# A decoder layer on one core: the gating's first factor moves from channel tiles to a ninth unit of seven-product block multiplication

## The chip, the cores and the metric

The kernel runs on one core of one Trainium2 chip. The core has TensorE (PE, matrix products; PEld is its weight load), VectorE (DVE), ScalarE (ACT), GpSimd (POOL) and SyncE (SP, whose queue issues the DMAs). Each engine works through its own instructions in order and waits for the others by semaphores. The metric is the device time of one execution in microseconds (us).

## The reference

One decoder layer with three gated branches, D_MODEL 2048, 256 positions, 256 memory tokens, all in float32. The part that the change touches is the branch with the spatial gating unit:

```python
proj = x @ w_in
q_a, k_a, v_a, z_a, u_g, v_g, z_g, q_c, z_c, g_logit = split(proj)
v = layer_norm(gelu(v_g));  mixed = masked 128x128 position mixing of v, + b_s
y_g = gelu(u_g) * mixed * silu(z_g)
merged = gates[0] * (y_a @ w_branch_attn) + gates[1] * (y_g @ w_branch_sgu) + gates[2] * (y_c @ w_branch_mem)
out = layer_norm(ALPHA * x + merged @ w_out)
```

`u_g`, the gating's first factor, is `x` (256 x 2048) times 1024 columns of `w_in`. The other two branches are attention over 8 heads (`q_a`, `k_a`, `v_a`, `z_a`) and cross-attention to the memory (`q_c`, `z_c`).

## The kernel before

Every product keeps nearly full float32 accuracy: each operand is split into a rounded part `hi` (a copy on ACT, L62) and a rest `lo` (a subtraction on DVE, L63), and the products hi*hi, hi*lo, lo*hi are summed in PSUM. So each weight that PE reads has passed ACT and DVE first.

Two streams of work share PE.

**The channel tiles** ("C"). A tile of 128 output columns (`channel_tile`) streams both parts of `x` past stationary weights: 16 steps of one 512-column matmul (hi, L190) and one 256-column matmul (lo, L191). Its weights come as one 1 MB chunk in `raw`, split in two halves of 1024 columns. `zc`, `qc`, `za`, `q`, `k`, `ug` and `zg` are eight such tiles each; `mv`, `mk` (the memory's values and keys) and the three gated branches `b` (12 matmuls of 512 columns in a half chunk) run on chunks too. PSUM tiles of these come from `acc`, three buffers.

**The block units** ("S"). A unit computes 1024 columns of `x @ w_in` as 2 x 2 blocks with seven products, M1 M5 M6 M3 M7 M4 M2. Each product is two steps (h = 0, 1) of 12 matmuls of 512 columns (L391 to L393), so a unit is 14 steps, numbered through all units. A step needs its block split into `sh` (ACT) and `sl` (DVE), 2048 columns each. Six steps of a unit need an in-place difference of two blocks on DVE first (`s_sum`, L312), and M3 two more (L325). The pool `shl` has four tiles, two pairs: the pair for step s + 2 can be written only when step s has left PE. Four results of a unit (128 x 512) are finished by an addition on DVE (L351). There are eight units: six for the merge gates, unit 2 for `v_a`, unit 5 for `v_g`.

The small matmuls of attention, memory attention, position mixing and the transposes of the merged result take turns in `aux`, two PSUM buffers. A buffer is reused in the order in which the program asks for one, so a tile waits for the tile two requests ahead. An attention head goes through three stages, scores (`s`), transposes (`pt`), values (`o`), one at each `tick` (one per finished C tile). The 256-wide work tiles (`q`, `k`, gates, halves of sums) share eight buffers `w1`.

What sets the order: `pace` assigns, from a table of DVE costs, how many S steps follow each C half (0 to 2), and `DUE` sets the latest places of whole units. The recorded program then passes a scheduler that builds each engine's final order, so S steps and C halves are interleaved matmul by matmul on PE. The first blocks of unit 0 are loaded as riders on given chunks (`riders`), among the loads of `mv` and `mk`.

At the end `u`, the GELU of `ug`, is multiplied into the mixed tile in `sgu_gate`, together with the SiLU of `zg`.

Of the kernel before, what the change touches and what calls it, by code (L numbers as in the profile page):

```python
# [10 lines left out]
AF = mybir.ActivationFunctionType  # L11
# [13 lines left out]


@with_exitstack
def decoder_layer(ctx, tc, xT, memT, x_tok, w_st, w_mv, w_mk, w_zc, w_qc, w_za, w_qk, w_ug, w_zg,
                  w_br, w_o, w_sT, sgu_bc, ln_g, ln_b, out):
    nc = tc.nc  # L30

# [10 lines left out]
    def w2(name, shape=(P, 512)):  # L42
        return work.tile(list(shape), F32, tag="w2", name=name, bufs=6)
# [4 lines left out]
    def spill(name, shape, dt=F32):  # L48
        return dram.tile(list(shape), dt, tag=name, name=name)
# [111 lines left out]
    chunks += [w_br[2 * 8 + j] for j in range(8)]  # L161
    chunks += [w_za[j] for j in range(3, 8)]
    chunks += [w_qk[j] for j in range(16)]
    chunks += [w_ug[j] for j in range(3)]
    chunks += [w_br[j] for j in range(8)]
    chunks += [w_ug[j] for j in range(3, 8)]
    chunks += [w_zg[j] for j in range(8)]
    chunks += [w_br[8 + j] for j in range(8)]

    def held(i, kh):  # L170
# [114 lines left out]

    UNITS = 8
    PRODUCTS = ("M1", "M5", "M6", "M3", "M7", "M4", "M2")
    FORM = {"M5": 1, "M6": 2, "M3": 4, "M7": 3}  # L290
    rt, shl, xsf, sp = {}, {}, {}, {}
# [161 lines left out]
    def run(gen):  # L453
# [5 lines left out]
        while left[0]:  # L459
# [1 line left out]
            yield  # L461

    first = lambda blk, h: lambda: s_load(0, blk, h)
    riders.update({4: [x_loads[0]], 5: [first(B12, 0)], 6: [x_loads[1]], 7: [first(B12, 1)],
                   10: [first(B11, 0)], 12: [first(B11, 1)]})
    for _ in run(mem_values()):
        pass
    for i, _ in enumerate(run(mem_keys())):
        if x_work:
            x_work.pop(0)()  # L470
        if i in (12, 14):
            riders[ptr["load"]] = [first(B22, i // 2 - 6)]
    while x_work:
        x_work.pop(0)()
        step(lambda: None)
# [20 lines left out]
                store(d[j], v)  # L496
            yield from channel_tile(x_k, f"{w}{j}", fin)

    szc_d, sza_d, gu_d = ([spill(f"{n}{j}", (P, S)) for j in range(8)] for n in ("szc", "sza", "gu"))


    MSC = float(2 * P) ** -0.5
# [148 lines left out]
    def sgu_gate(j):  # L651
        st = {}

        def fetch():
            st["c"] = w2(f"sc{j}", (P, 3, P))
            st["w"] = w1(f"ws{j}", (P, P))
            st["u"] = w1(f"gu{j}")
            nc.sync.dma_start(st["c"], sgu_bc[j].partition_broadcast(P))
            nc.sync.dma_start(st["w"], w_sT[:, j * P:(j + 1) * P])
            nc.sync.dma_start(st["u"], gu_d[j])  # L660
            nc.gpsimd.affine_select(out=st["w"], in_=st["w"], compare_op=ALU.is_ge,
                                    fill=0.0, base=0, pattern=[[1, P]], channel_multiplier=-1)

        def scale():
            v = vg[0][:, :, j * P:(j + 1) * P]
            for i, op in ((0, ALU.mult), (1, ALU.add)):
                nc.vector.tensor_tensor(v, v, st["c"][:, i][:, None, :].to_broadcast([P, 2, P]), op=op)

        def mix(z):
            ps = new_aux(f"mix{j}", (P, 2, P))  # L670
            for c in range(2):
                nc.tensor.matmul(ps[:, c], vg[0][:, c, j * P:(j + 1) * P], st["w"], start=(c == 0), stop=(c == 1),
                                 skip_group_check=True)
            m = w1(f"m{j}", (P, 2, P))
            nc.vector.tensor_tensor(m, ps, st["c"][:, 2][:, None, :].to_broadcast([P, 2, P]), op=ALU.add)
            m2 = m.rearrange("p c t -> p (c t)")
            nc.vector.tensor_tensor(m2, m2, st["u"], op=ALU.mult)
            nc.vector.tensor_tensor(m2, m2, z, op=ALU.mult)
            put_y(1, j, m2)

        return fetch, scale, mix

    def gating():
        for j in range(8):
            fetch, scale, mix = sgu_gate(j)
            fetch()

            def fin(ps, j=j, scale=scale, mix=mix):
                scale()
                z = w1(f"zg{j}")  # L690
                joined(z, ps, f"zg{j}")
                nc.scalar.activation(z, z, AF.Silu)
                pending.append([lambda: None, lambda: mix(z)])
            yield from channel_tile(x_k, f"zg{j}", fin)

# [64 lines left out]

    GATES = {0: (2, 0), 1: (2, 1), 3: (0, 0), 4: (0, 1), 6: (1, 0), 7: (1, 1)}

    def classic():
        yield from gate_tiles("zc", AF.Silu, szc_d)
        new_y(2)
        yield from mem_attention()
        yield from gate_tiles("za", AF.Silu, sza_d, range(3))
        yield from gated_branch(2, 0)
        yield from gate_tiles("za", AF.Silu, sza_d, range(3, 8))
        new_y(0)  # L770
        yield from block_attention()
        yield from gate_tiles("ug", AF.Gelu_apprx_tanh, gu_d, range(3))
        yield from gated_branch(0, 1)
        yield from gate_tiles("ug", AF.Gelu_apprx_tanh, gu_d, range(3, 8))
        new_y(1)
        yield from gating()
        yield from gated_branch(1, 2)

    S_STEPS = 14 * UNITS
    KINDS = ([(16, 1.2), (16, 1.75), (6, 1.2), (16, 1.3), (10, 1.2), (32, 1.65), (6, 1.2), (16, 1.6), (10, 1.2),
              (16, 2.2), (16, 1.9)])
    C_COST = [cost for n, cost in KINDS for _ in range(n)]
    DUE = {38: 14, 46: 28, 64: 42, 102: 56, 110: 70, 126: 84, 144: 98, 152: 112}
# [70 lines left out]
    for t in range(2):  # L856
        for i, c0 in enumerate((1536, 1792)):
# [83 lines left out]
```

## Time and profile before

| | |
|---|---|
| three runs: median (lowest to highest) | 997.91 us (997.07 to 998.18) |
| the profiled execution, its time | 1001.29 us |
| its span, first to last instruction | 999.5 us |
| PE busy | 977.3 us (98%) |
| DVE busy | 816.4 us (82%) |
| ACT busy | 592.8 us (59%) |
| HBM traffic over the span | 269 GB/s |
| TensorE clock granted, mean | 0.992 |

A busy share counts an instruction from its start to its end. Matmuls are pipelined: one of 512 columns is shown with 0.39 us, but the next starts 0.23 us later, so costs on PE are read as distances between starts. DVE instructions overlap by about 0.09 us in the same manner. A row of a timeline gives start, length, engine, line, operation, tiles written and read, and in brackets the idle time of the engine just before it and what ended it.

### The profile page before, as it was taken

Reading aid. Unit: us, or ns where it says so; the run is one execution under the profiler, and the core shown is the slowest. Engines: PE = TensorE matmul, PEld = TensorE weight load, DVE = VectorE, ACT = ScalarE, POOL = GpSimd, SP = SyncE. Lnnn points to the kernel's source line nnn. Section 1 sums busy time; section 2 is a strip of 40 time slices with the busy share of each in tenths; the row PEclk is TensorE's granted clock in tenths of the full one; section 3 lists DMA queues with packets and bytes.
Section 4 is the critical chain, followed back from the end, with each engine's and each line's share of the span. In section 5 each row is a group of like instructions: output and inputs, shape, how many; then the busy total and the mean of one; then the engine's idle time right before and its main releaser. Section 6 shows DMA issues by size and latency. Waiting matters only on the chain.

```text
span 999.5 us, 12911 instructions
## 1 busy us (share of the span) xinstructions
PE 977.3 (98%) x4888; PEld 824.2 (82%) x4888; DVE 816.4 (82%) x776; ACT 592.8 (59%) x669; POOL 6.4 (1%) x17
## 2 busy tenths in 40 slices
PE   9999999999999999999999999999999999999995
PEld 7778888888888888888888888877877888878885
DVE  5954998897689789788987988899899876676647
ACT  5644665546686565665566567886555557544520
POOL 0000000000000000000000000000000000000000
PEclk9999999999999999999999999999999999999998
DMA  9998579648974896697579468847986956868622
GB/s 334 405 397 322 208 254 397 230 174 290 339 260 159 332 400 229 241 348 269 178 289 363 143 238 322 311 162 304 404 304 216 342 176 207 284 234 320 227 82 84
DMA packets 68125, 269.28 MB, mean 269 GB/s; under 512 B 7520, under 2 KB 21600, under 8 KB 45536
## 3 DMA queue, kind: packets, MB, share of 16 engines
q1 hardware_dynamic: 68064, 268.47, 73.0%
q8 instruction: 38, 0.62, 0.2%
q14 instruction: 23, 0.19, 0.1%
HBM read 245.37 MB, written 23.07 MB: 269 GB/s over the span
## 4 chain that ended last, share of the span: by engine, by line
PE 86%; DVE 5%; ACT 4%; issue 3%; DMA 1%; SPq 0%; DVEq 0%; ACTq 0%
PE sM L392 9%; PE sM L391 9%; PE sM L393 9%; PE b L717 4%; PE b L718 4%; PE b L716 3%; PE mk L190 3%; PE zc L190 3%; PE za L190 3%; PE q L190 3%; PE qc L190 3%; PE zg L190 3%; PE o L824 3%; PE o L825 3%; PE o L823 3%; PE mv L429 3%
## 5 line engine op out<-in xcount | busy, mean ns | idle before, releaser
L63 DVE TENSOR_TENSOR lo<-raw,hi 128x1024 fp32r<-128x1024 f32 (+1 forms) x218 | 262.6, 1213 | 74.3 <-ACT hi L62 72.6
L62 ACT ACTIVATE hi<-raw 128x1024 fp32r<-128x1024 f32 (+1 forms) x218 | 227.0, 1048 | 156.2 <-PE o L825 31.9
L63 DVE TENSOR_TENSOR sl<-b,sh 128x2048 fp32r<-128x2048 f32 x112 | 256.1, 2290 | 53.3 <-ACT sh L62 53.1
L62 ACT ACTIVATE sh<-b 128x2048 fp32r<-128x2048 f32 x112 | 214.4, 1914 | 125.0 <-PE sM L392 107.5
L312 DVE TENSOR_TENSOR b<-b,b 128x2048 f32<-128x2048 f32 x48 | 109.8, 2288 | 9.9 <-DMA b<-in_w_st_dram 9.9
L392 PE MATMUL sM<-sl,xf 128*128 128x512 f32 x256 | 101.3, 396 | 0.9 <-DVE sl L63 0.9
L391 PE MATMUL sM<-sh,xf 128*128 128x512 f32 x256 | 100.7, 393 | 1.4 <-ACT sh L62 1.3
L393 PE MATMUL sM<-sh,xf 128*128 128x512 f32 x256 | 100.3, 392 | 0.0
L717 PE MATMUL b<-lo,yhl 128*128 128x512 f32 x192 | 75.4, 393 | 0.8 <-DVE lo L63 0.8
L391 PE MATMUL sM<-sh,xhl 128*128 128x512 f32 x192 | 75.7, 394 | 0.0
L392 PE MATMUL sM<-sl,xhl 128*128 128x512 f32 x192 | 75.5, 393 | 0.0
L393 PE MATMUL sM<-sh,xhl 128*128 128x512 f32 x192 | 75.0, 390 | 0.0
L718 PE MATMUL b<-hi,yhl 128*128 128x512 f32 x192 | 74.5, 390 | 0.0
L716 PE MATMUL b<-hi,yhl 128*128 128x512 f32 x192 | 72.2, 391 | 0.0
L391 PEld LDWEIGHTS sM<-sh,xf 128*128 128x128 f32 x256 | 48.1, 188 | 12.3 <-ACT sh L62 2.4
L392 PEld LDWEIGHTS sM<-sl,xf 128*128 128x128 f32 x256 | 48.1, 188 | 11.5 <-DVE sl L63 1.6
L393 PEld LDWEIGHTS sM<-sh,xf 128*128 128x128 f32 x256 | 48.1, 188 | 9.9
L190 PE MATMUL mk<-memhl,hi 128*128 128x512 f32 x128 | 46.1, 402 | 1.6 <-ACT hi L62 1.6
L190 PE MATMUL ug<-xhl,hi 128*128 128x512 f32 x128 | 47.3, 406 | 0.0
L190 PE MATMUL q<-xhl,hi 128*128 128x512 f32 x128 | 46.8, 399 | 0.0
L190 PE MATMUL k<-xhl,hi 128*128 128x512 f32 x128 | 46.7, 399 | 0.0
L190 PE MATMUL qc<-xhl,hi 128*128 128x512 f32 x128 | 46.1, 399 | 0.0
(295 smaller groups left out, 1886.2 us busy)
## 6 DMA issues: line engine op xcount, KB each, us to landing
b<-in_w_st_dram SPq DMA_DIRECT2D x64, 1024.0 KB, 7.4
xf<-xf SPq DMA_DIRECT2D x64, 512.0 KB, 5.3
raw<-in_w_br_dram SPq DMA_DIRECT2D x24, 1024.0 KB, 5.2
raw<-in_w_qk_dram SPq DMA_DIRECT2D x16, 1024.0 KB, 7.0
raw<-in_w_o_dram SPq DMA_DIRECT2D x16, 1024.0 KB, 4.9
raw<-in_w_mk_dram SPq DMA_DIRECT2D x8, 1024.0 KB, 9.1
raw<-in_w_zc_dram SPq DMA_DIRECT2D x8, 1024.0 KB, 5.5
raw<-in_w_qc_dram SPq DMA_DIRECT2D x8, 1024.0 KB, 6.4
```

The source lines that it names most:

```text
L62: nc.scalar.activation(hi, v, AF.Copy)
L63: nc.vector.tensor_tensor(lo, v, hi.bitcast(F32), op=ALU.subtract)
L190: nc.tensor.matmul(ps, hi, x, start=first, stop=False)
L312: nc.vector.tensor_tensor(o, rt[u, other, h], o, op=ALU.subtract)
L391: nc.tensor.matmul(ps, ah, hi[:, c], start=first, stop=False, skip_group_check=True)
L392: nc.tensor.matmul(ps, ah, lo[:, c], start=False, stop=False, skip_group_check=True)
L393: nc.tensor.matmul(ps, al, hi[:, c], start=False, stop=last, skip_group_check=True)
L429: nc.tensor.matmul(ps[t][n], lhs, rhs[:, n * 512:(n + 1) * 512], start=(k == 0 and rhs is hi and lhs is xh[t]), stop=(k == KT - 1 and lhs ...
L716: nc.tensor.matmul(ps[t], yh, hi[:, c], start=(k == 0), stop=False)
L717: nc.tensor.matmul(ps[t], yh, lo[:, c], start=False, stop=False)
L718: nc.tensor.matmul(ps[t], yl, hi[:, c], start=False, stop=(k == 7))
L823: nc.tensor.matmul(ps[:, 0:n], mh, hi, start=first, stop=False)
```

## The change

`ug` is no longer eight channel tiles. Its 1024 columns become unit 6 of the block units, between `v_g` and the gates of the gating branch, so there are 9 units and 126 S steps instead of 8 and 112. A unit's results have positions on the partitions, and the gating wants channels there, so each of the four results (128 x 512) is transposed on PE in four 128 x 128 pieces into an `aux` tile (`channel_major`), GELU is applied as ACT reads it, and it is stored. `sgu_gate` fetches it in two pieces and multiplies it into the SiLU of `zg` (`both`) instead of into the mixed tile.

Where `ug`'s first three tiles stood, ahead of the gated branch 0, `zg`'s first three tiles are computed now, stored in `szg`, and fetched again in `gating` (`behind`); `gating` computes the other five.

The table of the pace, the due places and the tail limit are set anew, and unit 0's first blocks ride on other chunks.

```diff
-    riders.update({4: [x_loads[0]], 5: [first(B12, 0)], 6: [x_loads[1]], 7: [first(B12, 1)],
-                   10: [first(B11, 0)], 12: [first(B11, 1)]})
+    riders.update({4: [x_loads[0]], 6: [x_loads[1]], 9: [first(B12, 0)], 11: [first(B12, 1)],
+                   13: [first(B11, 0)], 14: [first(B11, 1)], 16: [first(B22, 0)], 17: [first(B22, 1)]})
...
-        if i in (12, 14):
-            riders[ptr["load"]] = [first(B22, i // 2 - 6)]
...
-            nc.vector.tensor_tensor(m2, m2, st["u"], op=ALU.mult)
...
+        def both(z):
+            nc.vector.tensor_tensor(z, z, st["u"], op=ALU.mult)
...
+        elif u == 6:
+            late.append(lambda: channel_major(t, n, r))
...
+    def channel_major(t, n, r):
+        ps = new_aux(f"uT{t}{n}", (P, 4, P))
+        for i in range(4):
+            nc.tensor.transpose(ps[:, i], r[:, i * P:(i + 1) * P], ident)
+        v = w2(f"uv{t}{n}", (P, 4, P))
+        nc.scalar.activation(v, ps, AF.Gelu_apprx_tanh)
+        store(gu_d[t, n], v)
...
-        yield from gate_tiles("ug", AF.Gelu_apprx_tanh, gu_d, range(3))
+        yield from gate_tiles("zg", AF.Silu, szg_d, range(3))
         yield from gated_branch(0, 1)
-        yield from gate_tiles("ug", AF.Gelu_apprx_tanh, gu_d, range(3, 8))
...
-    DUE = {38: 14, 46: 28, 64: 42, 102: 56, 110: 70, 126: 84, 144: 98, 152: 112}
+    DUE = {38: 14, 46: 28, 64: 42, 102: 56, 110: 70, 114: 84, 118: 98, 128: 112, 136: 126}
```

Three places show what becomes of the order. Names end in a buffer number; a line of the kernel after stands one lower than the same line before.

ACT, where `mv` ends and `mk` begins, before (`mvs` is the copy of a finished `mv` tile, `hi8_0` the first half of `mk`'s first chunk):

```order
L62 ACTIVATE xw10_782<-F10_749 128x4x128
L62 ACTIVATE xw11_807<-F11_750 128x4x128
L439 ACTIVATE mvs01_491<-mv01_122 128x512
L439 ACTIVATE mvs11_495<-mv11_124 128x512
L62 ACTIVATE hi8_0_434<-raw8_344 128x1024
L62 ACTIVATE hi8_1_450<-raw8_344 128x1024
```

and now:

```order
L62 ACTIVATE xw11_809<-F11_752 128x4x128
L62 ACTIVATE hi8_0_430<-raw8_340 128x1024
L62 ACTIVATE hi8_1_446<-raw8_340 128x1024
L438 ACTIVATE mvs01_489<-mv01_122 128x512
L62 ACTIVATE hi9_0_467<-raw9_376 128x1024
```

Both halves of `mk`'s first chunk have moved ahead of the two copies that wait for the last `mv` matmuls.

PE, around S steps 82 to 84, before (`ug2` is a C tile, `o6`, `s7` belong to attention heads 6 and 7):

```order
L392 MATMUL sM2_5_5382<-sl82_5305,xhl_96 128x512
...
L190 MATMUL ug2_5449<-xhl_96,hi66_1_5399 128x512
L191 MATMUL ug2_5449<-xhl_96,lo66_1_5400 128x256
L608 MATMUL o6_5315<-ptT6_5245,vah6_5147 128x256
...
L579 MATMUL s7_5321<-kT7_5059,qT7_5058 128x256
L392 MATMUL sM2_5_5382<-sl83_5353,xhl_96 128x512
...
L391 MATMUL sM1_6_5475<-sh84_5395,xhl_96 128x512
L190 MATMUL ug2_5449<-xhl_96,hi66_1_5399 128x512
```

and now, from the end of `k6` to the first matmul of `q7`, the next C tile:

```order
L390 MATMUL sM2_5_4564<-sh82_4484,xhl_96 128x512
...
L190 MATMUL k6_5505<-xhl_96,lo61_1_5428 128x256
L391 MATMUL sM2_5_4564<-sl82_4485,xhl_96 128x512
...
L390 MATMUL sM1_6_4673<-sh93_5056,xf93_5054 128x512
L778 MATMUL uT01_5134<-ident_83,k6_6_4997 128x128 x4
L599 MATMUL pt3_5163<-ident_83,p3_5074 128x128 x3
L390 MATMUL sM4_6_5236<-sh94_5154,xhl_96 128x512
...
L606 MATMUL o3_5258<-ptT3_5167,vah3_5085 128x256
...
L390 MATMUL sM4_6_5236<-sh95_5205,xhl_96 128x512
L189 MATMUL q7_5601<-xhl_96,hi62_0_5506 128x512
```

Steps 82 to 94, thirteen of them, stand in one piece, with no C matmul between; the transposes of head 3 stand behind `uT01`, the first transposes of the new unit, and `q7` behind both.

DVE, between the splits of steps 85 and 88, before (`lo68`, `lo69` are halves of C chunks):

```order
L312 TENSOR_TENSOR b0_6_1_5263<-b1_6_1_5122,b0_6_1_5263 128x2048
L63 TENSOR_TENSOR sl86_5492<-b0_6_0_5193,sh86_5491 128x2048
L640 BN_STATS vst_5472<-vg_5174 128x6
L63 TENSOR_TENSOR lo68_0_5564<-raw68_5403,hi68_0_5563 128x1024
L211 TENSOR_TENSOR ug2_5536<-ug2_5449,ug2l_5537 128x256
L63 TENSOR_TENSOR lo68_1_5617<-raw68_5403,hi68_1_5616 128x1024
L325 TENSOR_TENSOR b1_6_1_5122<-b2_6_1_5356,b1_6_1_5122 128x2048
L63 TENSOR_TENSOR lo69_0_5653<-raw69_5499,hi69_0_5652 128x1024
L312 TENSOR_TENSOR b0_6_0_5193<-b2_6_0_5308,b0_6_0_5193 128x2048
L644 BN_AGGR vmv_5473<-vst_5472 128x2
L63 TENSOR_TENSOR sl87_5533<-b0_6_1_5263,sh87_5532 128x2048
```

and now:

```order
L324 TENSOR_TENSOR b1_6_0_4267<-b2_6_0_4488,b1_6_0_4267 128x2048
L63 TENSOR_TENSOR sl86_4690<-b0_6_0_4356,sh86_4689 128x2048
L311 TENSOR_TENSOR b0_6_1_4400<-b1_6_1_4312,b0_6_1_4400 128x2048
L642 BN_AGGR vmv_4672<-vst_4671 128x2
L311 TENSOR_TENSOR b0_6_0_4356<-b2_6_0_4488,b0_6_0_4356 128x2048
L324 TENSOR_TENSOR b1_6_1_4312<-b2_6_1_4528,b1_6_1_4312 128x2048
L217 TENSOR_SCALAR vgv_4847<-vmv_4672 128x2
L63 TENSOR_TENSOR sl87_4731<-b0_6_1_4400,sh87_4730 128x2048
L63 TENSOR_TENSOR sl88_4793<-b0_6_0_4356,sh88_4792 128x2048
```

The halves of C chunks have left this stretch; splits of S steps and differences of blocks follow each other directly.

## Rows read from the trace of the kernel before

**Rows 1.** Stretches: length, busy time of engines, clock, DMA share (columns in the header).

```profile
core 0: us, PE busy (x) PEld busy (x) DVE busy (x) ACT busy (x) POOL busy (x), PEclk, DMA share, GB/s
101.00:605.40 504.40, 504.40 (x2536) 427.07 (x2535) 438.51 (x351) 314.88 (x351) 0.00 (x0) 1.00 0.73 266
647.40:734.00 86.60, 84.61 (x371) 68.43 (x370) 82.66 (x71) 59.27 (x61) 0.00 (x0) 1.00 0.79 307
734.00:786.40 52.40, 49.41 (x246) 41.34 (x245) 50.70 (x45) 30.39 (x30) 0.00 (x0) 0.97 0.74 261
```

**Rows 2.** Groups by line: operation, tiles, count, busy us, mean ns, idle before.

```profile
L63 DVE TENSOR_TENSOR sl<-b,sh 128x2048 fp32r<-128x2048 f32 x112 | 256.1, 2290 | 53.3 <-ACT sh L62 53.1
L62 ACT ACTIVATE sh<-b 128x2048 fp32r<-128x2048 f32 x112 | 214.4, 1914 | 125.0 <-PE sM L392 107.5 <-DVE b L312 7.6 <-PE sM L393 4.4
L312 DVE TENSOR_TENSOR b<-b,b 128x2048 f32<-128x2048 f32 x48 | 109.8, 2288 | 9.9 <-DMA b<-in_w_st_dram 9.9
L190 PE MATMUL ug<-xhl,hi 128*128 128x512 f32 x128 | 47.3, 406 | 0.0
L351 DVE TENSOR_TENSOR k<-sM,k 128x512 f32<-128x512 f32 x32 | 22.0, 686 | 2.5 <-PE sM L393 2.3
```

**Rows 3.** Timeline of PE: distances between starts in each kind of work.

```profile
642.77 0.39 PE L190 MATMUL ug<-xhl,hi 128*128 128x512 f32 x1
...
644.17 0.40 PE L190 MATMUL ug<-xhl,hi 128*128 128x512 f32 x1
...
746.28 0.39 PE L391 MATMUL sM<-sh,xf 128*128 128x512 f32 x1
...
747.64 0.39 PE L391 MATMUL sM<-sh,xf 128*128 128x512 f32 x1
...
904.57 1.03 PE L744 MATMUL mT<-ident,sg 128*128 128x128 f32 x8
905.36 0.48 PE L824 MATMUL o<-lo,mhl 128*128 128x512 f32 x1
```

**Rows 4.** PE and ACT where mk begins, the clock behind it, mk's first loads.

```profile
51.37 0.61 PE L429 MATMUL mv<-hi,memhl 128*128 128x512 f32 x2
53.62 0.49 PE L190 MATMUL mk<-memhl,hi 128*128 128x512 f32 x1 [1.63 <-ACT hi L62]
54.88 0.39 PE L191 MATMUL mk<-memhl,lo 128*128 128x256 f32 x1 [0.76 <-DVE lo L63]
...
51.12 0.60 ACT L439 ACTIVATE mvs<-mv 128x512 f32<-128x512 f32 x1 [4.18 <-PE mv L429]
...
52.52 1.05 ACT L62 ACTIVATE hi<-raw 128x1024 fp32r<-128x1024 f32 x1
...
56.00:60.00 4.00, 4.00 (x15) 3.42 (x15) 1.09 (x1) 1.03 (x1) 0.00 (x0) 0.59 1.01 404
...
L125 SPq DMA_DIRECT2D raw<-in_w_mk_dram x3: 328/332/333, 37.3 to 48.2; - x3
...
DMA to landing us min/median/max: 5.3/10.4/11.3
```

**Rows 5.** PE and DVE around PE's longest wait, and the clock behind it.

```profile
751.38 0.39 PE L191 MATMUL ug<-xhl,lo 128*128 128x256 f32 x1 [2.67 <-DVE lo L63]
...
743.17 2.29 DVE L63 TENSOR_TENSOR sl<-b,sh 128x2048 fp32r<-128x2048 f32 x1
745.37 2.29 DVE L325 TENSOR_TENSOR b<-b,b 128x2048 f32<-128x2048 f32 x1
...
750.10 1.23 DVE L63 TENSOR_TENSOR lo<-raw,hi 128x1024 fp32r<-128x1024 f32 x1
...
753.03 0.63 PE L190 MATMUL ug<-xhl,hi 128*128 128x512 f32 x1
...
754.31 0.63 PE L190 MATMUL ug<-xhl,hi 128*128 128x512 f32 x1
...
753.00:755.00 2.00, 2.00 (x9) 1.71 (x8) 2.00 (x2) 0.00 (x0) 0.00 (x0) 0.50 0.59 115
```

More of the change, by code (lines that the diff above doesn't have):

```diff
@@ L27, in decoder_layer @@
 @with_exitstack
-def decoder_layer(ctx, tc, xT, memT, x_tok, w_st, w_mv, w_mk, w_zc, w_qc, w_za, w_qk, w_ug, w_zg,
+def decoder_layer(ctx, tc, xT, memT, x_tok, w_st, w_mv, w_mk, w_zc, w_qc, w_za, w_qk, w_zg,
                   w_br, w_o, w_sT, sgu_bc, ln_g, ln_b, out):
@@ L163, in decoder_layer @@
     chunks += [w_qk[j] for j in range(16)]
-    chunks += [w_ug[j] for j in range(3)]
+    chunks += [w_zg[j] for j in range(3)]
     chunks += [w_br[j] for j in range(8)]
-    chunks += [w_ug[j] for j in range(3, 8)]
-    chunks += [w_zg[j] for j in range(8)]
+    chunks += [w_zg[j] for j in range(3, 8)]
     chunks += [w_br[8 + j] for j in range(8)]
@@ L283, in decoder_layer @@
     x_loads, x_work = x_stages()
-    UNITS = 8
+    UNITS = 9
     PRODUCTS = ("M1", "M5", "M6", "M3", "M7", "M4", "M2")
@@ L497, in gate_tiles @@
             yield from channel_tile(x_k, f"{w}{j}", fin)
-    szc_d, sza_d, gu_d = ([spill(f"{n}{j}", (P, S)) for j in range(8)] for n in ("szc", "sza", "gu"))
+    szc_d, sza_d, szg_d = ([spill(f"{n}{j}", (P, S)) for j in range(8)] for n in ("szc", "sza", "szg"))
+    gu_d = {(t, n): spill(f"gu{t}{n}", (P, 4, P)) for t in range(2) for n in range(2)}
     MSC = float(2 * P) ** -0.5
@@ L654, in fetch @@
         def fetch():
-            st["c"] = w2(f"sc{j}", (P, 3, P))
-            st["w"] = w1(f"ws{j}", (P, P))
+            sc = w2(f"sc{j}", (P, 4, P))
+            st["c"], st["w"] = sc[:, 0:3], sc[:, 3]
             st["u"] = w1(f"gu{j}")
@@ L659, in fetch @@
             nc.sync.dma_start(st["w"], w_sT[:, j * P:(j + 1) * P])
-            nc.sync.dma_start(st["u"], gu_d[j])
+            for t in range(2):
+                nc.sync.dma_start(st["u"][:, t * P:(t + 1) * P], gu_d[t, j // 4][:, j % 4])
             nc.gpsimd.affine_select(out=st["w"], in_=st["w"], compare_op=ALU.is_ge,
@@ L676, in mix, with behind, fin @@
             m2 = m.rearrange("p c t -> p (c t)")
-            nc.vector.tensor_tensor(m2, m2, st["u"], op=ALU.mult)
             nc.vector.tensor_tensor(m2, m2, z, op=ALU.mult)
             put_y(1, j, m2)
-        return fetch, scale, mix
+        def both(z):
+            nc.vector.tensor_tensor(z, z, st["u"], op=ALU.mult)
+        return fetch, scale, both, mix
     def gating():
-        for j in range(8):
-            fetch, scale, mix = sgu_gate(j)
+        def behind(j):
+            fetch, scale, both, mix = sgu_gate(j)
             fetch()
-            def fin(ps, j=j, scale=scale, mix=mix):
+            z = w1(f"szg{j}")
+            nc.sync.dma_start(z, szg_d[j])
+            pending.append([lambda: (scale(), both(z)), lambda: mix(z)])
+        for j in range(3, 8):
+            fetch, scale, both, mix = sgu_gate(j)
+            fetch()
+            if j < 6:
+                late.append(lambda j=j: behind(j - 3))
+            def fin(ps, j=j, scale=scale, both=both, mix=mix):
                 scale()
@@ L692, in fin @@
                 nc.scalar.activation(z, z, AF.Silu)
+                both(z)
                 pending.append([lambda: None, lambda: mix(z)])
@@ L759, in s_finish @@
                 pending.append(sgu_norm())
-    GATES = {0: (2, 0), 1: (2, 1), 3: (0, 0), 4: (0, 1), 6: (1, 0), 7: (1, 1)}
+    def channel_major(t, n, r):
[5 more added lines that the diff above has]
+        store(gu_d[t, n], v)
+    GATES = {0: (2, 0), 1: (2, 1), 3: (0, 0), 4: (0, 1), 7: (1, 0), 8: (1, 1)}
     def classic():
@@ L781, in decoder_layer @@
     S_STEPS = 14 * UNITS
-    KINDS = ([(16, 1.2), (16, 1.75), (6, 1.2), (16, 1.3), (10, 1.2), (32, 1.65), (6, 1.2), (16, 1.6), (10, 1.2),
-              (16, 2.2), (16, 1.9)])
+    KINDS = ([(16, 1.2), (16, 1.75), (6, 1.2), (16, 1.3), (10, 1.2), (32, 1.65), (6, 1.9), (16, 1.8), (10, 2.2),
+              (16, 1.9)])
     C_COST = [cost for n, cost in KINDS for _ in range(n)]
-    DUE = {38: 14, 46: 28, 64: 42, 102: 56, 110: 70, 126: 84, 144: 98, 152: 112}
+    DUE = {38: 14, 46: 28, 64: 42, 102: 56, 110: 70, 114: 84, 118: 98, 128: 112, 136: 126}
     S_COST = 3.2
@@ L801, in decoder_layer @@
     share = 0.80
-    while pace(share)[1] < S_STEPS or sum(pace(share)[0][:148]) < S_STEPS:
+    while pace(share)[1] < S_STEPS or sum(pace(share)[0][:134]) < S_STEPS:
         share += 0.005
@@ L863, in decoder_layer @@
         normalise(t)
-_ARGS = ['xT', 'memT', 'x_tok', 'w_st', 'w_mv', 'w_mk', 'w_zc', 'w_qc', 'w_za', 'w_qk', 'w_ug', 'w_zg',
+_ARGS = ['xT', 'memT', 'x_tok', 'w_st', 'w_mv', 'w_mk', 'w_zc', 'w_qc', 'w_za', 'w_qk', 'w_zg',
          'w_br', 'w_o', 'w_sT', 'sgu_bc', 'ln_g', 'ln_b']
@@ L902, in _layout @@
         "x_tok": a["x"].reshape(2, P, D),
-        "w_st": np.stack([blocks(w) for w in (gate(2, 0), gate(2, 1), col(2), gate(0, 0), gate(0, 1), col(5),
+        "w_st": np.stack([blocks(w) for w in (gate(2, 0), gate(2, 1), col(2), gate(0, 0), gate(0, 1), col(5), col(4),
                                               gate(1, 0), gate(1, 1))]),
@@ L910, in _layout @@
         "w_qk": np.stack([q, k], 1).reshape(16, P, D),
-        "w_ug": stat(col(4)),
         "w_zg": stat(col(6)),
```

## Prediction

> **What bounds the kernel now.** First the table of stretches [rows 1]: from 101 to 605 us PE is busy for the whole 504.4 us while DVE is busy for 438.5 (87%). PE is the bound there and loses nothing to waits, though DVE has only 13% to spare. The next two stretches differ: from 647 to 734 PE stands idle for 2.0 us (86.60 less 84.61) with DVE at 95%, and from 734 to 786 for 3.0 us (52.40 less 49.41) with DVE at 97%. So DVE becomes the bound wherever the work that PE asks of it is dense, and PE waits there. The timeline shows one case [rows 5]: `lo` of a `ug` half stands behind a row of 2048-wide splits and differences, starts at 750.10, and PE waits 2.67 us for it; afterwards the granted clock is 0.50, which is 1.2 instead of 2.4 GHz. The other loss lies where `mv` gives way to `mk` [rows 4].
>
> **Costs of one piece.** On PE a pair of a C step costs 0.35 us (four pairs between 642.77 and 644.17), a matmul of an S step 0.227 us (six between 746.28 and 747.64), a transpose 0.10 us (eight between 904.57 and 905.36) [rows 3]. An S step, 12 matmuls, is thus 2.73 us of PE. On DVE a 2048-wide operation lasts 2.29 us, but the next starts 2.20 us later (743.17 to 745.37) [rows 2, 5]; taking off the same 0.09, a `lo` costs 1.14 (1.23 in [rows 5]) and a result's addition 0.60 (0.686 in [rows 2]). A unit has 14 splits, 8 differences and 4 additions: 22 times 2.20 plus 4 times 0.60 is 50.8 us of DVE, or 3.63 per step. That is more than the 2.73 of PE that the step gives: S steps can run at PE's speed only mixed with C steps, which cost PE 2.80 per half and DVE only 1.14 and a little.
>
> **The change, part by part.**
>
> *The work on PE.* Away go 128 pairs of `ug`, counted in [rows 2]: 128 times 0.35 is 44.8 us. New are 14 steps of 2.73, 38.2 us, and 16 transposes of 0.10, 1.6 us. Sum: -5.0 us, on the path wherever PE is the bound. The bounds are -5.5 (transposes hidden) and -2.4 (a transpose at the 0.26 us that is left of its busy time if nothing overlaps, from the 1.03 of [rows 3]).
>
> The Trainium skill, "TensorE: Matmul & The Clock Gate", Part 4, gives about 275 ns for a transpose in a kernel's context. Here eight start within 0.79 us, so by the trace they overlap; with the page's figure 16 would cost 4.4 us and this item would be -2.2.
>
> *The order where `mk` begins.* Before, ACT copies two `mv` tiles, idle for 4.18 us until PE has finished them, and only then rounds `mk`'s first chunk at 52.52. PE starts a matmul at 51.60 and the next at 53.62: 1.8 us lost; the following one at 54.88: 1.0 lost; then the clock is at 0.59 for 4 us, some 1.5 lost [rows 4]. Sum 4.3. Now both halves stand ahead of the copies. Their data was there even before: the load issued at 37.3 landed at the latest 11.3 us on, at 48.6 [rows 4], and 2 MB of riders are now behind it. I take -4.3; bounds -4.5 and -2.
>
> *The waits between 647 and 787.* They sum to 5.0 us of idle PE [rows 1], and the half clock behind the longest costs some 1.4 (a clock of 0.97 over 52.4 us): 6.4. These places exist no longer in this form. What stands there now is costed next, so I take the whole -6.4 out and put +3 in for waits of the same kind at the new places (0 to 6): the plan has 12 S steps in 16 halves of branch 0 as before, and about as much DVE work as PE work in `gating` (five tiles, three sets of `behind` and three S steps: some 40 us on either).
>
> *The thirteen S steps in one piece.* In PE's order now, steps 82 to 94 follow each other without a C matmul. The reason is in the code: `uT01` asks for an `aux` buffer two requests ahead of head 3's later tiles, so head 3's transposes cannot pass it; it needs the result of M3 of unit 6 (steps 90, 91); and behind head 3 the work and PSUM buffers of `k5` and with them `q7` are held. In the order before, C tiles and attention stand between the same steps. So DVE's and PE's work are summed from the end of `sl83` to the end of `sl94`. DVE has 11 splits and 8 differences, 19 times 2.20, 41.8 us, and some 6.1 of others (an estimate from rows: four additions or statistics of 0.60, one `lo` of 1.14, the gating norm's two 1024-wide scalings and its small operations, 2.6 together): 47.9. PE has 11 steps, 30.0 us, and about 1.4 of transposes and attention: 31.4. DVE has no lead to bring in, since the pair for step 83 is free only after step 81 and ACT's 1.91 and DVE's 2.29 follow [rows 2], while step 82 alone (2.73) covers them. The deficit is 16.5. Added to that are places where DVE itself waits for ACT: in M3 and M7 no difference stands between the splits, so `sl91` must wait until step 89 has left PE and `sh91` is done (2.5 us for the rest of the step, 1.9 for ACT, of which `sl90` covers 2.2). Going through the thirteen steps one by one with these durations I get 3.5 us of such waits: 20.0 in all. The longest single wait is near 6 us, before `sl87`, behind a split and four differences. After waits of 2 to 3 us the clock fell towards half [rows 4, 5]; while PE waits for DVE anyhow that costs little, and I take no more for it. So +20; bounds 14 (DVE keeps a lead of one split) and 28 (half clock through the run).
>
> *The rest.* ACT does 14 roundings of 1.91 more and is busy 62% in 101 to 605 [rows 1]: hidden. `both` replaces one DVE product by another; the `szg` spill adds three small stores and loads. SP carries eight reloads of the x sums (0.5 MB) more, with DMA at 0.73 in the long stretch [rows 1]: hidden, and a late block would cost as much as one of today's (9.9 us of DVE idle in all, [rows 2], none of which PE felt before 605). The first block loads come some chunks later but before their first use in `zc`; nothing.
>
> **Sum.** -5.0 - 4.3 - 6.4 + 3 + 20 = +7.3. The profiled execution took 1001.3 us, 1.8 of it outside its span of 999.5, so its like would take 1008.6. It lies 3.4 above the median of the runs, and on the scale of the median 997.9 + 7.3 gives 1005.2. I predict **1005 us**.
>
> **The rivals.**
>
> *The run of S steps is paid back, no change.* The C halves held back in the run (`q7`, `k7`, `zg`) come in a bunch afterwards and ask little of DVE, so it may regain a lead and the later waits (+3) vanish; with the run at its sum of 16.5 the time is 997.9 - 15.7 + 16.5 = 998.7. For it: 101 to 605 went without loss at 87%. Against it: the two pairs of `shl` allow no lead of more than two steps.
>
> *Faster: the run costs only a few us.* If DVE came into step 82 two steps ahead and the differences of M5 and M6 were done under C halves, only a part of the deficit would reach PE. It decides at 12.7 us for the run (5.0 + 4.3 + 6.4 - 3), where the change gives back all that it gains; at 6 the time is 997.9 - 12.7 + 6 = 991.2. For it: the saving on PE is certain, and the opening's stall is removed by order alone. Against it: `shl`, and the differences of one unit cannot start before the splits of the same blocks.
>
> *Slower still.* If the granted clock stays at half through the run, PE becomes the slower one: at a clock of 0.50 two pairs of a C step take from 753.03 to 754.31, 0.64 each instead of 0.35 [rows 5], so a step takes 2.73 times 0.64 / 0.35, 5.0 us, against DVE's 4.4 there (47.9 over 11): 13 times 0.6 on top, 8, and 1013. Against it: PE would have to stay unworked for long enough again and again; in the trace full clock is back within 4 us [rows 4].
>
> **How the numbers follow.** The forecast (1000 to 1010) has 0.60, slower still 0.08, no change 0.14, faster 0.18. The range, 992 to 1013, reaches from the fast rival's time to the slow one's and takes in the bounds of the run with the other terms at their values (1005.2 - 6 = 999 and 1005.2 + 8 = 1013); outside it lie about 0.1 of the chance below and 0.06 above. A difference under 0.2%, 2.0 us, can't be told from none in this kernel. So faster 0.18, same 0.14, slower 0.68.
>
> **What would show it.** In the profile after: `mk` starts right behind `mv` with no wait and no fall of the clock near 55 us (if not, +4.3). PE shows idle time of 15 us or more within some 55 us shortly after 570, released by DVE's `sl`, with DVE busy throughout; the transposes of head 3 behind it; and a lower clock in parts of it. Matmuls of unit 6 stand 0.227 apart elsewhere. If PE has less than 10 us of idle time there, the step on the run is wrong and the change is a gain; if the wait is released by a DMA or by ACT, the mechanism is another.

## The result, and the profile after

The changed kernel takes 1014.14 us (median of 4 runs, 1012.46 to 1017.74), the kernel before, beside it, 997.74: a ratio of 1.0155, 95% interval 1.0124 to 1.0186. It is slower, as forecast, but by 16 us instead of 7; 1014 lies 1.1 us above the range. The profiled execution took 1015.7 us, its span is 1014.0.

Engines over the whole span (page, part 1: busy us, share, instructions), then stretches to be held against [rows 1] and [rows 4]:

```profile
PE 981.2 (97%) x4816; PEld 820.8 (81%) x4816; DVE 843.5 (83%) x778; ACT 597.7 (59%) x655; POOL 11.6 (1%) x17
```

```profile
core 0: us, PE busy (x) PEld busy (x) DVE busy (x) ACT busy (x) POOL busy (x), PEclk, DMA share, GB/s
53.60:62.00 8.40, 8.40 (x51) 7.35 (x50) 4.72 (x7) 5.05 (x8) 0.00 (x0) 1.00 1.03 420
76.00:101.00 25.00, 22.49 (x117) 18.92 (x117) 9.64 (x11) 10.75 (x12) 0.00 (x0) 0.93 0.97 383
101.00:605.40 504.40, 504.09 (x2511) 425.58 (x2510) 445.29 (x344) 315.88 (x339) 0.00 (x0) 1.00 0.74 276
609.00:662.00 53.00, 41.21 (x154) 29.91 (x153) 49.29 (x38) 30.16 (x24) 0.00 (x0) 0.90 0.47 168
750.00:800.00 50.00, 46.55 (x200) 36.58 (x199) 47.68 (x36) 31.08 (x30) 0.00 (x0) 1.00 0.77 283
```

The first, second and fourth of these stretches in the kernel before:

```profile
53.60:62.00 8.40, 7.62 (x33) 6.39 (x34) 4.72 (x4) 2.95 (x4) 0.00 (x0) 0.80 0.99 362
76.00:101.00 25.00, 25.00 (x146) 22.00 (x144) 12.57 (x13) 12.71 (x15) 0.00 (x0) 1.00 0.84 323
609.00:662.00 53.00, 52.94 (x261) 44.11 (x260) 47.30 (x46) 44.60 (x57) 0.00 (x0) 1.00 0.73 267
```

Where `mk` begins (53.6 to 62) PE loses nothing and the clock is 1.00, as forecast. But at `mk`'s end (76 to 101) PE stands for 2.5 us and its clock is 0.93; before, the same stretch had PE busy for 25.00 at 1.00. The long middle is without loss. From 609 to 662 lies most of the run of S steps: 154 matmuls, at 0.227 some 35.0 us of work, took 53.0 us, so 18 us are lost, with DVE busy for 49.3. Some 15 of the 154 are narrow ones (transposes and attention), which take less than 0.227, so the loss is nearer to 20; the kernels below are counted in the same way.

The run in PE's timeline, its longer waits, the sum of all waits from 605 to 662 (who waited for whom: us, times, longest), and the clock in its middle:

```profile
613.67 0.50 PE L391 MATMUL sM<-sl,xhl 128*128 128x512 f32 x1 [1.16 <-DVE sl L63]
618.55 0.50 PE L390 MATMUL sM<-sh,xf 128*128 128x512 f32 x1 [1.82 <-ACT sh L62]
623.74 0.50 PE L391 MATMUL sM<-sl,xf 128*128 128x512 f32 x1 [2.18 <-DVE sl L63]
630.22 0.49 PE L390 MATMUL sM<-sh,xf 128*128 128x512 f32 x1 [1.58 <-ACT sh L62]
632.69 0.79 PE L391 MATMUL sM<-sl,xf 128*128 128x512 f32 x1 [1.98 <-DVE sl L63]
```

```profile
PE sM L391 <- DVE sl L63: 7.4, 8, 2.2
PE sM L390 <- ACT sh L62: 4.4, 4, 1.8
```

```profile
620.00:630.00 10.00, 6.30 (x19) 3.91 (x18) 10.00 (x6) 4.25 (x3) 0.00 (x0) 0.83 0.11 32
630.00:640.00 10.00, 7.80 (x21) 5.98 (x22) 9.86 (x13) 4.05 (x5) 0.00 (x0) 0.66 0.17 54
```

11.8 us of the loss are shown as waits. Of the rest, the lower clock in these two stretches, behind waits of up to 2.2 us (for part of each it is 1.2 instead of 2.4 GHz), makes some 3.7 (0.17 of 6.30 and 0.34 of 7.80 busy us), and the end of the last matmul before each of the twelve waits counts as busy (0.39 shown, 0.23 of it work). DVE is busy throughout 620 to 640: three of the four waits named after ACT (3.6 of their 4.4 us) stand behind DVE too, since `sh` of a differenced block waits for the difference.

The end of `mk`: PE, then ACT, then SP, whose rows are the issues of DMAs:

```profile
93.95 0.50 PE L189 MATMUL mk<-memhl,hi 128*128 128x512 f32 x1 [1.42 <-ACT hi L62]
95.21 0.39 PE L190 MATMUL mk<-memhl,lo 128*128 128x256 f32 x1 [0.76 <-DVE lo L63]
```

```profile
79.02 2.01 ACT L62 ACTIVATE hi<-raw 128x1024 fp32r<-128x1024 f32 x2 [3.31 <-DMA raw<-in_w_mk_dram]
84.25 2.01 ACT L62 ACTIVATE hi<-raw 128x1024 fp32r<-128x1024 f32 x2 [2.95 <-DMA raw<-in_w_mk_dram]
```

```profile
68.47 0.49 SPq L297 DMA_DIRECT2D b<-in_w_st_dram  x1
69.16 0.73 SPq L408 DMA_DIRECT2D mk<-mk  x1
72.24 0.33 SPq L125 DMA_DIRECT2D raw<-in_w_mk_dram  x1
73.51 0.33 SPq L297 DMA_DIRECT2D b<-in_w_st_dram  x1
74.85 0.33 SPq L408 DMA_DIRECT2D mk<-mk  x1
75.22 1.54 SPq L321 DMA_DIRECT2D xf<-xf  x2
78.96 0.32 SPq L509 DMA_DIRECT2D mkh<-mk  x1
81.45 0.33 SPq L125 DMA_DIRECT2D raw<-in_w_mk_dram  x1
```

These are the two waits that stood at `mk`'s beginning before (1.63 and 0.76 in [rows 4]); they have moved to its last chunk. That chunk is issued at 81.45, when the block load issued at 68.47 has landed, and lands itself at 92.4 (before: issued at 78.2, landed at 85.5); ACT waited for the two chunks ahead of it as well. In front of it stand the riders (`b<-in_w_st_dram`), with DMA at 0.97 to 1.03. `zc` begins at 102.5 us, before at 100.9.

### The profile page after: what moved, and what is told of

Its sections match the earlier page's. It is cut to its first block, busy times and chain, and to the rows that moved or that the text cites. A ratio compares the mean times of both kernels' runs of the same rounds, so it can differ in the third digit from the quotient of the medians.

```text
span 1014.0 us, 12779 instructions
## 1 busy us (share of the span) xinstructions
PE 981.2 (97%) x4816; PEld 820.8 (81%) x4816; DVE 843.5 (83%) x778; ACT 597.7 (59%) x655; POOL 11.6 (1%) x17
## 4 chain that ended last, share of the span: by engine, by line
PE 78%; DVE 10%; DMA 4%; issue 4%; ACT 2%; SPq 0%; DVEq 0%; ACTq 0%
PE sM L391 10%; PE sM L392 10%; PE sM L390 9%; PE b L729 3%; PE b L730 3%; PE b L728 3%; DVE sl L63 3%; PE za L189 3%; PE q L189 3%; PE qc L189 3%; PE k L189 3%; PE o L846 3%; PE o L845 3%; PE o L844 3%; PE mv L428 3%
## 5 line engine op out<-in xcount | busy, mean ns | idle before, releaser
L63 DVE TENSOR_TENSOR sl<-b,sh 128x2048 fp32r<-128x2048 f32 x126 | 288.2, 2290 | 61.9 <-ACT sh L62 58.4
L62 ACT ACTIVATE sh<-b 128x2048 fp32r<-128x2048 f32 x126 | 241.1, 1914 | 151.1 <-PE sM L391 123.1
L62 ACT ACTIVATE hi<-raw 128x1024 fp32r<-128x1024 f32 (+1 forms) x202 | 210.5, 1047 | 152.3 <-PE o L846 30.6
L63 DVE TENSOR_TENSOR lo<-raw,hi 128x1024 fp32r<-128x1024 f32 (+1 forms) x202 | 243.0, 1212 | 67.7 <-ACT hi L62 63.8
L391 PE MATMUL sM<-sl,xf 128*128 128x512 f32 x288 | 116.7, 405 | 7.6 <-DVE sl L63 7.6
L390 PE MATMUL sM<-sh,xf 128*128 128x512 f32 x288 | 115.2, 400 | 3.6 <-ACT sh L62 3.6
L392 PE MATMUL sM<-sh,xf 128*128 128x512 f32 x288 | 114.4, 397 | 0.0
L390 PE MATMUL sM<-sh,xhl 128*128 128x512 f32 x216 | 85.0, 394 | 0.8 <-ACT sh L62 0.8
L392 PE MATMUL sM<-sh,xhl 128*128 128x512 f32 x216 | 84.5, 391 | 0.0
L390 PEld LDWEIGHTS sM<-sh,xf 128*128 128x128 f32 x288 | 54.9, 191 | 16.9 <-ACT sh L62 5.2
L392 PEld LDWEIGHTS sM<-sh,xf 128*128 128x128 f32 x288 | 55.1, 191 | 11.0
L391 PEld LDWEIGHTS sM<-sl,xhl 128*128 128x128 f32 x216 | 40.6, 188 | 11.1 <-DVE sl L63 3.1
L390 PEld LDWEIGHTS sM<-sh,xhl 128*128 128x128 f32 x216 | 40.6, 188 | 9.4 <-ACT sh L62 1.1
L392 PEld LDWEIGHTS sM<-sh,xhl 128*128 128x128 f32 x216 | 40.6, 188 | 7.9
```

What stands on the lines that cost most here:

```text
L62: nc.scalar.activation(hi, v, AF.Copy)
L63: nc.vector.tensor_tensor(lo, v, hi.bitcast(F32), op=ALU.subtract)
L390: nc.tensor.matmul(ps, ah, hi[:, c], start=first, stop=False, skip_group_check=True)
L391: nc.tensor.matmul(ps, ah, lo[:, c], start=False, stop=False, skip_group_check=True)
L392: nc.tensor.matmul(ps, al, hi[:, c], start=False, stop=last, skip_group_check=True)
```

## The experiments

Times are medians; "before" was run beside each group (998.8, 998.5 and 999.1 us), and ratios are to it. Diffs are against the changed kernel unless said otherwise.

| kernel | us | ratio to before (95%) |
|---|---|---|
| changed kernel | 1014.14 | 1.0155 (1.0124 to 1.0186) |
| own buffers | 1004.92 | 1.0053 (1.0035 to 1.0071) |
| PSUM tile only | 1020.50 | 1.0207 (1.0184 to 1.0231) |
| aux kept, work tile freed | 1013.45 | 1.0141 (1.0122 to 1.0161) |
| no differences in unit 6 | 1003.21 | 1.0047 (1.0031 to 1.0063) |
| old riders | 1014.27 | 1.0154 (1.0132 to 1.0176) |
| kernel before, new riders | 1002.59 | 1.0034 (1.0021 to 1.0046) |
| riders between | 1027.59 | 1.0286 (1.0263 to 1.0309) |
| own buffers, riders in the gap | 1004.47 | 1.0052 (1.0035 to 1.0069) |
| own buffers, old riders | 1006.12 | 1.0074 (1.0052 to 1.0095) |
| the same, earlier plan | 1004.05 | 1.0057 (1.0041 to 1.0073) |
| gap riders and earlier plan | 1008.47 | 1.0094 (1.0077 to 1.0111) |
| own buffers, no differences in unit 8 | 993.25 | 0.9938 (0.9923 to 0.9953) |

### What holds the C tiles back

```diff
-        ps = new_aux(f"uT{t}{n}", (P, 4, P))
+        ps = psum.tile([P, 4, P], F32, tag="sps", name=f"uT{t}{n}", bufs=3)
...
-        v = w2(f"uv{t}{n}", (P, 4, P))
+        v = r.rearrange("p (a b) -> p a b", a=4)
```

Both hunks (own buffers):

> The transposes of the new unit take their PSUM tile from the S steps' own buffers (sps) instead of aux, and GELU writes back into the result's own tile instead of one of the shared work tiles; nothing else changes. In PE's order C halves and S steps then alternate again through steps 82 to 94. Theory A (the run of thirteen S steps costs PE about 20 us, and shared buffers hold the C tiles back): the 18 to 20 us of PE waits between 605 and 662 us fall to under 6, some 2 to 4 come back where DVE is dense behind zg, and the time is 996 to 1000 us. Rival B (DVE simply has too much work for this stretch, the run is only where it shows): the waits move to other places, above all to 700 to 800 us, and the time stays at 1009 to 1014 us.

The first hunk alone:

> Only the PSUM tile of the new transposes is moved (from aux to sps); the GELU result still takes a shared 512-wide work tile (w2). The prediction's reason (aux alone holds the attention heads and with them q7): the run of S steps is gone, 996 to 1000 us. Rival (either shared buffer is enough, since the scheduler lets C run ahead until one of its heads needs a buffer that a late S result has asked for first): twelve S steps still stand in one piece, PE waits 15 to 20 us there, and the time is 1011 to 1015 us.

The second alone:

> The changed kernel with the GELU result written back into the result's own tile instead of a shared 512-wide work tile; the transposes stay in aux. If aux alone is enough to hold C back (the prediction's reason, as one of two sufficient ones): thirteen S steps in one piece, 18 to 20 us of waits at 605 to 662 us, 1013 to 1016 us. If the shared work tile is the only holder: run gone, 1003 to 1006 us.

The stretch of the run, 609 to 662 us, in these three, in this order (of the first also 700 to 750 and 800 to 850):

```profile
609.00:662.00 53.00, 53.00 (x277) 45.12 (x276) 48.52 (x50) 39.39 (x49) 0.00 (x0) 1.00 0.52 188
700.00:750.00 50.00, 46.92 (x203) 36.91 (x202) 48.08 (x37) 33.33 (x31) 0.00 (x0) 1.00 0.75 273
800.00:850.00 50.00, 42.86 (x201) 34.58 (x200) 48.86 (x55) 29.84 (x34) 22.05 (x3) 0.97 0.70 247
```

```profile
609.00:662.00 53.00, 38.91 (x147) 28.55 (x145) 49.05 (x35) 28.70 (x23) 0.00 (x0) 0.90 0.46 164
```

```profile
609.00:662.00 53.00, 41.30 (x155) 30.05 (x154) 49.42 (x38) 30.26 (x25) 0.00 (x0) 0.90 0.47 172
```

With both shared buffers freed the run is gone: PE is busy for all of the 53 us, with C tiles in it. With either of the two left it is there, and as dear as in the changed kernel (147 and 155 matmuls at 0.227: 19.6 and 17.8 us lost, as 18 there). So the prediction's reason, `aux`, is sufficient but not the whole: the shared 512-wide work tiles, of which each attention head takes two (`p` and `ptT`), hold C back just as well. That 1020.5 came out of freeing `aux` alone, 5 us over what its rival theory said, is not explained; its trace only shows where: against the changed kernel PE stands 2.3 us longer from 605 to 662, 3.3 longer from 750 to 800 and 1.3 longer before 605.

With own buffers the gain, 9 us, is half of what was lost in the run, so the time lies between the two theories: waits came back at 700 to 750 (3.1 us) and 800 to 850 (7.1 us), with DVE at 96% and 98%. PE's program order shows why. S steps issued when a stretch of C begins:

| | three `zg` tiles | branch 0 | rest of `zg` | last branch | all |
|---|---|---|---|---|---|
| before (first column: `ug`) | 77 | 85 | 106 | 111 | 112 |
| changed | 99 | 104 | 120 | 123 | 126 |
| own buffers | 86 | 91 | 107 | 116 | 126 |

Held back, C lets S catch up by 13 steps early; not held back, the same steps come late, among work that loads DVE as well.

### Is it DVE's work?

```diff
-        if other is not None:
+        if other is not None and u != 6:
...
-            sub(b(B12), b(B22), b(B12))
+            if u != 6:
+                sub(b(B12), b(B22), b(B12))
```

> The changed kernel without the eight differences of blocks of the new unit (left out: DVE's 2048-wide subtractions b for unit 6, so its products take undifferenced blocks). PE's order keeps thirteen S steps in one piece; DVE has 8 times 2.20 = 17.6 us less to do within it. Theory A (in the run DVE's work is the bound, 47.9 us against PE's 31.4): DVE then needs 30.3, less than PE, only the waits for ACT remain, PE's waits between 605 and 665 us fall from 20 to 6 to 9 and the time is 997 to 1002 us. Rival (the two pairs of split buffers and ACT's rounding in front of each split set the pace): the waits stay at 14 or more and the time is 1007 us or more.

The run ends 11 us earlier here: `q7` begins at 652.8 us instead of 664.1 (a stretch of the run, and PE's waits from 605 to 662):

```profile
609.00:645.00 36.00, 30.36 (x127) 22.58 (x126) 29.32 (x26) 23.83 (x19) 0.00 (x0) 1.00 0.50 178
```

```profile
PE sM L392 <- DVE sl L63: 5.6, 6, 1.2
```

11 us less for 17.6 us of DVE. The longest wait is 1.2 us and the clock stays at 1.00, but 127 matmuls (28.8 us) still take 36, so 7 us stay although DVE has only 29.3 us of work. The time lies between the two theories: DVE's load makes the larger part. The rest is put down to the chain of PE, ACT and DVE over two pairs of buffers (3.5 us in the prediction), which no run isolates. The profiled run took 1008.0, 4.8 over the median.

The same edit for unit 8 (`u != 8`), on own buffers:

> Own buffers as in the first experiment, and the eight differences of blocks of unit 8, the last, left out (its products take undifferenced blocks): DVE has 17.6 us less to do from about 770 to 850 us. If the waits that came back there are DVE's again: PE's waits from 775 to 875 us fall from 11 to under 4 and the time is 994 to 998 us. If they belong to something else at the end of the branches (small products, buffers): the waits stay at 8 or more, 1002 to 1005 us.

```profile
800.00:850.00 50.00, 50.00 (x243) 42.11 (x242) 44.45 (x58) 36.05 (x39) 1.92 (x2) 1.00 0.83 308
```

The 7.1 us of waits (not 11, as the expectation had it) are gone and the time falls by 11.7 to 993.25: what came back at 800 to 850 is DVE's again; the 3.1 us at 700 to 750, ahead of this unit, stay. (Both kernels leave work out, so neither is a better one.)

### The first block loads

The riders as before (first hunk of the change undone):

> The changed kernel with unit 0's first block loads where they were before. Theory R (the later loads push back mk's own last chunks, which costs PE about 6 us at the end of mk; the order at its beginning gains about 4): PE has no wait between 76 and 101 us, again loses about 4 us at 51 to 60 us, zc begins within 1 us of 101 us, and the time is 1011 to 1014 us. Rival (as the prediction had it, the later loads cost nothing and the order gains 4.3): 1017 to 1019 us, with zc beginning near 106 us.

The kernel before with that hunk alone:

> The kernel before with nothing changed but the riders, set as in the changed kernel. The prediction costed this part at -4.3 us: 993 to 995 us. By the changed kernel's trace the gain at the beginning of mk is given back at its end (4.3 gained, 5 to 6 lost): zc begins near 102 us, 998 to 1001 us.

The two ends of `mk`, old riders first, then the kernel before with new riders:

```profile
53.60:62.00 8.40, 7.47 (x32) 6.21 (x33) 4.72 (x4) 3.08 (x4) 0.00 (x0) 0.80 0.98 355
76.00:101.00 25.00, 25.00 (x146) 22.05 (x145) 12.41 (x12) 12.71 (x15) 0.00 (x0) 1.00 0.84 326
```

```profile
53.60:62.00 8.40, 8.40 (x49) 7.16 (x48) 6.01 (x8) 4.63 (x7) 0.00 (x0) 1.00 0.99 383
76.00:101.00 25.00, 22.51 (x125) 18.91 (x125) 10.53 (x13) 9.85 (x13) 0.00 (x0) 1.00 0.99 399
```

The stall goes with the riders: old riders, stall at the beginning (clock 0.80) and none at the end; new riders, the reverse, in either kernel. `zc` begins at 101.1 and 102.8. The part that was forecast at -4.3 us costs 2.1 to 4.6 in the kernel before (spans: +1.4), its time 1.6 over what was expected from the changed kernel's trace, and undoing it in the changed kernel changes nothing that can be told (1014.27; spans: -1.7). One trace alone is good to about a microsecond here: in the seven traces with the new riders `zc` begins at 100.4 to 102.8, in the four with the old ones at 100.0 to 101.6.

Riders between the two settings:

```diff
-    ... 6: [x_loads[1]], 9: [first(B12, 0)], 11: [first(B12, 1)],
-    13: [first(B11, 0)], 14: [first(B11, 1)], 16: [first(B22, 0)], 17: [first(B22, 1)]
+    ... 5: [first(B12, 0)], 6: [x_loads[1]], 9: [first(B12, 1)],
+    11: [first(B11, 0)], 13: [first(B11, 1)], 17: [first(B22, 0)], 18: [first(B22, 1)]
```

> The changed kernel with the two B12 loads on chunks 5 and 9, B11 on 11 and 13, B22 on 17 and 18: mk's first chunk is still rounded ahead of the two mv copies, but less is queued ahead of mk's last chunks. Theory R: both stalls of the opening are small, zc begins between 97 and 100 us instead of 102.5, and the time is 1008 to 1012 us (the run of S steps, here fourteen, is left as it is). Rival (DMA is saturated in the opening, so any placing costs the same bytes): zc begins at 101 to 103 us, 1013 to 1016 us.

```profile
54.27 0.38 PE L190 MATMUL mk<-memhl,lo 128*128 128x256 f32 x1 [1.45 <-DVE lo L63]
72.67 0.49 PE L189 MATMUL mk<-memhl,hi 128*128 128x512 f32 x1 [1.42 <-ACT hi L62]
73.93 0.39 PE L190 MATMUL mk<-memhl,lo 128*128 128x256 f32 x1 [0.77 <-DVE lo L63]
```

Both theories missed. `mk` stalls in its beginning, its middle and its end (from 76 to 101 PE is busy for 22.8 us), and `zc` begins at 104.6. The rest of the 13 us lies later, in a run of fourteen steps among other places: the scheduler's order behind the opening had moved.

Own buffers, with these riders:

```diff
-    ... 9: [first(B12, 0)], 11: [first(B12, 1)],
-    13: [first(B11, 0)], 14: [first(B11, 1)], 16: [first(B22, 0)], 17: [first(B22, 1)]
+    ... 8: [first(B12, 0)], 9: [first(B12, 1)],
+    11: [first(B11, 0)], 13: [first(B11, 1)], 17: [first(B22, 0)], 18: [first(B22, 1)]
```

> Own buffers as in the first experiment (1004.9 us, zc begins at 101.4), and unit 0's first block loads on chunks 8, 9, 11, 13, 17 and 18 instead of 9, 11, 13, 14, 16 and 17: one load moves into the stretch from 40 to 50 us, where DMA is busy only 0.60 in the changed kernel, and two behind mk's last chunk. Theory R (block loads queued ahead of mk's last chunks stall PE at the end of mk; DMA is full from 50 to 92 us): no stall at either end of mk, zc begins at 96 to 98.5 us, 999 to 1001.5 us. Rival (any placing only moves the stall): zc begins at 101 us or later, 1003 to 1006 us.

```profile
53.60:62.00 8.40, 8.40 (x51) 7.35 (x50) 4.70 (x7) 4.86 (x8) 0.00 (x0) 1.00 1.02 420
76.00:101.00 25.00, 24.60 (x139) 20.95 (x139) 13.84 (x14) 13.89 (x15) 0.00 (x0) 1.00 0.95 369
...
800.00:850.00 50.00, 42.75 (x175) 33.82 (x174) 43.87 (x44) 29.79 (x33) 0.00 (x0) 0.90 0.64 231
```

For the opening theory R holds: with one megabyte moved into the gap and less ahead of `mk`'s last chunks all but 0.4 us of both stalls is gone, and `zc` begins at 98.5, 2.9 us earlier than with own buffers alone and 2.4 earlier than before. (In the last kernel below, with the same riders, it begins at 96.5, 4.4 earlier than before: the gain that was forecast for the opening was there to be had.) The total did not follow; it lies in the rival's range. From `zc` on it takes 3.2 us longer: other riders, another order, and now 13 S steps stand in the last branch, where the clock is 0.90.

### Spreading the S steps

Own buffers with old riders:

> Own buffers as in the first experiment (1004.9 us), and unit 0's first block loads on their old chunks as well. If the loads only move one stall of the opening from the end of mk to its beginning: zc begins near 101 us, no wait at 76 to 101, and the time is 1003 to 1005.5 us. If the later loads cost something of their own: 998 to 1001 us. PE's waits from 700 to 850 us stay at 12 to 16 us.

That kernel with one number of the plan changed:

```diff
-    while pace(share)[1] < S_STEPS or sum(pace(share)[0][:134]) < S_STEPS:
+    while pace(share)[1] < S_STEPS or sum(pace(share)[0][:120]) < S_STEPS:
```

> The kernel of the experiment before it, with one number of the plan changed: all S steps are to be planned by C half 120 instead of 134, so some of them come earlier, where DVE has 10 to 14 per cent to spare. If the 10 us of waits after 700 us are only the lag of the S stream being caught up late: 2 to 5 us less than with the old limit, 999 to 1002 us. If DVE is so full over the whole of zc to the last branch that the waits only move: within 1 us of it.

Own buffers and gap riders, with a plan that asks for S steps earlier still (beside the limit, 130, the table of costs, and a bound on the lag, -4.0 instead of -2.0):

```diff
-    DUE = {38: 14, 46: 28, 64: 42, 102: 56, 110: 70, 114: 84, 118: 98, 128: 112, 136: 126}
+    DUE = {28: 14, 40: 28, 56: 42, 92: 56, 104: 84, 110: 98, 122: 112, 128: 126}
```

> The kernel of the experiment before it, with the plan set to bring S steps earlier (due places 4 to 10 C halves earlier, DVE costs of a C half 1.4 to 1.75 instead of 1.2 to 2.2, limit 130). If the waits after 700 us can be spread into the stretches where DVE has room: 2 to 5 us under that kernel, 995 to 999 us, which would be level with the kernel before or a little better. If the waits only move: within 1 us of it.

1006.1, 1004.1 and 1008.5: the first 0.6 us over the expected range, with 12.4 us of waits from 700 to 850, as expected; the second 2 us better, the least that its expectation named, with intervals that overlap; the third 4 us worse than the kernel that it starts from, which neither theory had. PE's order shows that the edits don't do what they say: in all three some 86 S steps stand ahead of the first `zg` tiles and 12 in the last branch. With all three plans the scheduler lets C run ahead as far as buffers allow. The third has the longest wait of all:

```profile
825.73 0.80 PE L390 MATMUL sM<-sh,xf 128*128 128x512 f32 x1 [6.60 <-ACT sh L62]
```

No version beats the kernel before; a plan that holds C back evenly was not found.

## Why the prediction missed by 9 us

**What held.** The direction, the place of the run in PE's order and what bounds it; in time it came at 607 us, not shortly after 570. From `zc`'s start to the end the spans differ by +12.9 us (898.6 before, 911.5 after); the terms for that part sum to -5.0 - 6.4 + 3 + 20 = +11.6. The run cost 18 to 20 (154 matmuls in 53 us) against 20. The later waits are near 4 (3.5 of them from 750 to 800) against 3. That leaves -3 to -5 for PE's own work, forecast as -5.0. The transposes cost what the trace of before said: four start within 0.43 us:

```profile
654.70 0.60 PE L778 MATMUL uT<-ident,k 128*128 128x128 f32 x4
655.13 0.49 PE L599 MATMUL pt<-ident,p 128*128 128x128 f32 x3
```

**The step that failed: "The first block loads come some chunks later but before their first use in `zc`; nothing."** I looked at who needs the loads, not at what they are queued ahead of. DMA was at 1.01 from 56 to 60 already in [rows 4], so a megabyte that leaves one place must take time at another, and it took it from `mk`'s last chunks. With it the opening's -4.3 became +1.6 (`zc` at 102.5 instead of 100.9): 5.9 us, good to about one. The gain itself came, at 53 us, and was given back at 94. The two experiments that swap the riders alone show that the stall goes with them, and the riders in the gap that the gain stays when less stands in front of those chunks.

**The scale.** The profiled run of before lay 3.4 us over its median, that of after 1.6: another 1.8. With the 1.3 from `zc` on this is 9.0 of 9.1 us.

**Right size, other make-up.** The one wait near 6 us before `sl87` came as several of up to 2.2, and 11.8 us of idle PE is less than the 15 that I named; the clock that I counted at nothing (3.7 us) and the ends of matmuls in front of the waits (some 2) made up most of the difference. **Right place, half a reason:** `aux` is one of two holders.

**The rivals.** "Paid back" needed the later waits to vanish; they are near 4 us. "Faster" needed DVE to bring a lead into the run; PE's first wait stands 7 us into it (613.67, the last C matmul at 606.73). "Slower still" needed half clock throughout: the clock fell to 0.83 and 0.66 in 20 us only. The prediction treated the run as a cost of its own. The own-buffer kernel shows that half of it is a debt: those S steps pressed on DVE in every place where they were put here. Taken as a loss that is avoided by freeing the buffers, +20 would have been 10 too much.

## What to carry to other kernels

A load that moves is costed at what it is queued ahead of: where DMA is full, count the megabytes in front of the next chunk that somebody waits for. A shared rotating buffer orders the streams that share it; when a new user is added, list all shared pools that it asks, since freeing one of two brought nothing here. And a stretch in which a second engine is the bound is no loss that a new order removes by itself: ask where that engine has room, and whether the order can reach it.

## What the runs showed of the hardware

SP's issues showed a limit that I had not counted on: at 81.45 it issued when the eighth DMA back (68.47, the rows above) landed, and at 84.18 when that of 72.24 did; between 74 and 95 us it waited 13.7 us for the landing of earlier DMAs, with old riders 4.2. The trace has the reason: this program gives SP's 488 DMAs eight semaphores in turn, so the limit is the program's, and no run shows one of the chip. Since DMA stayed full meanwhile (1.02 from 60 to 90 us), it is the bytes in front that delayed the chunk. In the full stretch (60 to 70 us) 420 GB/s were moved, loads and stores together. The Trainium skill, "DMA: Bandwidth & Descriptors", section "Where 436 GB/s comes from", names about 358 GB/s per core as what binds loads from HBM and 435 as the ceiling of the fabric; the trace sits close under the second, so the measurement decides for it here, for this kernel on one core.

The transposes of the new unit are shown with 272 ns each, near the 275 ns of the Trainium skill, "TensorE: Matmul & The Clock Gate", Part 4 (given there beside a figure for bf16, here float32), but start 0.11 us apart: the page's figure is a length here, not the price of one in a row.
